# Transposing the gated convolution input, group A's output and the queries and keys on VectorE, quadrant by quadrant

## The chip, the cores and the metric

The kernel runs on one core of one Trainium2 chip. The metric is device time in microseconds (us) of one execution. TensorE (PE) multiplies matrices and writes to PSUM; VectorE (DVE) and ScalarE (ACT) work elementwise; GpSimd (POOL) does a few small powers; SyncE (SP) issues the DMAs. Each engine works through its own queue in order.

## The reference, cut to what matters

A trunk of two layers on a sequence of 256 tokens (two tiles of 128, here called token tiles) with 2048 channels in float32. Each layer:

```python
h = rmsnorm(x, norm_mix_pre[l])
proj = h @ w_in[l]                      # 2048 -> 5120 columns
a_q, a_k, a_v, b_glu, c_q, c_k, c_v, d_q, d_k, d_v = jnp.split(proj, split_at, axis=-1)
out_a = diff_attention(a_q, a_k, a_v, diff_lambda[l], diff_subln[l], l)   # 4 heads, rotary
out_b = conformer_conv(b_glu, conv_dw[l], ...)     # a*sigmoid(g), 31-tap depthwise conv, layernorm, silu, 512x512
out_c = gqa_axial_attention(c_q, c_k, c_v, ...)    # 4 query heads, 2 key heads
out_d = neighbourhood_attention(d_q, d_k, d_v, na_rpb[l])                 # 4 heads
mixed = jnp.concatenate([out_a, out_b, out_c, out_d], axis=-1) @ w_out[l]
x = x + rmsnorm(mixed, norm_mix_post[l])
h = rmsnorm(x, norm_ffn_pre[l])
f = (jax.nn.silu(h @ ffn_gate[l]) * (h @ ffn_up[l])) @ ffn_down[l]
x = x + rmsnorm(f, norm_ffn_post[l])
```

## The kernel before, in words

Every large product is made of three products of rounded float32 halves: high times high, high times low, low times high. A weight block of 128 rows by 1024 columns (a *unit*) is loaded, ACT writes its high half (`whi`), DVE the low half (`wlo`), and PE takes both. A *step* is one unit against one token tile: six matmuls of 128x512. Each layer goes through four phases in a fixed order of steps: the input projection (160 steps, in the column pairs B, C, A, D, V: `IN_ORDER`), the output projection (64 steps; its first half takes the groups' outputs in the order C, B, A, D: `OUT_ORDER`), gate and up, and down.

The order of all instructions is written by a planner while the kernel is built. `run` walks over the steps. Before each step it calls `fill` (convolution taps for DVE), `tick` (lets each running side job, a Python generator, go on to its next `yield`), `splits_to` (high and low halves, up to 7 units ahead) and `fill` again. `lhs` looks whether the left operand of the step has been made; as long as it hasn't, `wait` advances the planner's PE clock by 0.2 us and lets side jobs run, without a matmul of the step in between. So an output of group B that is late in the program stands ahead of all later steps on PE.

The planner keeps a clock for each engine in `spend` (lines 158 to 177). A DVE instruction is entered with 0.07 (or 0.13) us plus its elements per partition divided by 960, a PE transpose with 0.107 us. A side job may go on only when the planner's PE clock has passed the end of what it issued last plus 0.4 us (`LATENCY`, line 41). `fill` (line 339) issues taps only while DVE's clock is less than 1.5 us (`CONV_LEAD`, line 40) ahead of PE's.

The side jobs that the change touches:

- `glu` (line 644): after the column pair B, for each token tile, a times sigmoid(g); four PE transposes into a PSUM bank of the pool `tp`, an ACT copy into `uT`. When both token tiles are there, `conv` (line 671) issues the 31 taps for 4 channel blocks on DVE (`taps`), then for each token tile `conv_norm` (PE transposes, ACT, DVE, POOL, PE transposes, four ACT activations), then four products with `conv_pw`, which give `mixB`.
- `attn_a`, `attn_c`, `attn_d` (lines 808, 887, 958): after the column pairs A, C and D, `heads_transposed` turns queries and keys: per round one claim of a `tp` bank, four (or two) PE transposes, one ACT copy. There are 4 rounds in A, 4 in C (two of them of two blocks), 4 in D. Then the heads follow, at most two at a time.
- `out_a` (line 1013): when the four heads of A are done and the values V are there, for each token tile the products with the values, a norm, four PE transposes, and the split into `mixA`.

The pool `tp` has two PSUM banks; a job that finds both claimed yields until one is free.

`post` (line 541 and above) already turns the fourth quarter of x on DVE, as sixteen transposes of 32 partitions x 4 blocks x 32, four between two yields. The same form of instruction is what the change uses.

Of the kernel before, what the change touches and what calls it, by code (L numbers as in the profile page):

```python
# [13 lines left out]
AF = mybir.ActivationFunctionType  # L14
# [5 lines left out]
P = 128  # L20
L = 2
S = 256
T = S // P
# [7 lines left out]
PAD = TAPS // 2  # L31
# [71 lines left out]
class Trunk:  # L103
# [461 lines left out]
    def turned(self, l, j):  # L565
# [10 lines left out]
        for tok in range(T):  # L576
            self.mark("h", l, j, tok)


    def layer_consts(self, l):  # L580

        nc, a = self.nc, self.a
        lc = self.slot([2048], F32, "lc")
        v = self.v = {}
        self.l = l
        at = 0

        def part(n, shape):
            nonlocal at
            w = int(np.prod(shape))  # L590
            t = lc[:, at:at + w]
            at += w
            if len(shape) > 1:
                names = "abc"[:len(shape)]
                t = t.rearrange(f"p ({' '.join(names)}) -> p {' '.join(names)}", **dict(zip(names, shape)))
            v[n] = t
            return t

        for n in ("gqa_q_norm", "gqa_k_norm", "diff_subln"):
            part(n, (HD,))  # L600
        nc.sync.dma_start(lc[:, 0:at], a["heads"][l].partition_broadcast(P))
        first = at
        part("dw", (4, TAPS))
        for n in ("conv_dw_b", "conv_ln_g", "conv_ln_b", "conv_pw_b"):
            part(n, (4,))
        nc.sync.dma_start(lc[:, first:at], a["conv"][l])
        yield
        yield
        nc.vector.tensor_scalar(part("subln", (HD,)), v["diff_subln"], 1.0 - self.lam_init(l), None,
                                op0=ALU.mult)  # L610
        for n in ("q", "k"):
            g = v[f"gqa_{n}_norm"]
            cg, sg = part(f"cos_{n}", (T, HD)), part(f"sin_{n}", (T, HD))
            nc.vector.tensor_tensor(cg, self.rope["cos_c"], g.unsqueeze(1).to_broadcast([P, T, HD]),
                                    op=ALU.mult)
            gv = g.rearrange("p (b h w) -> p b h w", b=2, h=2)
            s4 = self.rope["sin_c"].rearrange("p t (b h w) -> p t b h w", b=2, h=2)
            o4 = sg.rearrange("p t (b h w) -> p t b h w", b=2, h=2)
            for h in range(2):
                for t in range(T):  # L620
                    nc.vector.tensor_tensor(o4[:, t, :, h], s4[:, t, :, h], gv[:, :, 1 - h], op=ALU.mult)
# [22 lines left out]
    def glu(self, phase, pair, tok):  # L644
        nc = self.nc
        if tok == 0:
            self.u = self.slot([T, 512], F32, "u")
            self.uT = self.slot([4, S + 2 * PAD], F32, "uT")
            nc.gpsimd.memset(self.uT[:, :, 0:PAD], 0.0)
            nc.gpsimd.memset(self.uT[:, :, PAD + S:], 0.0)  # L650
        av, gv = (self.acc[phase, pair, tok, b] for b in range(2))
        r = self.rstd[:, tok:tok + 1]
        u = self.u[:, tok]
        nc.scalar.activation(u, gv, AF.Sigmoid, scale=r)
        nc.vector.scalar_tensor_tensor(u, av, r, u, op0=ALU.mult, op1=ALU.mult)
        yield
        yield from self.claim("tp")
        b = self.bank("tp", (4, P))
        for c in range(4):
            nc.tensor.transpose(b[:, c], u[:, c * P:(c + 1) * P], self.ident)  # L660
        yield
        nc.scalar.activation(self.uT[:, :, PAD + tok * P:PAD + (tok + 1) * P], b, AF.Copy)
        yield
        self.free("tp")
        self.mark("u", phase)
        if tok == T - 1:
            yield from self.until(T, "u", phase)
            yield
            yield from self.conv()
# [103 lines left out]
            yield from self.until(T, "a", phase)  # L773
            yield from self.attn_a()

    def heads_transposed(self, dst, src, n):

        nc = self.nc
        for tok in range(T):
            yield from self.claim("tp")  # L780
            b = self.bank("tp", (4, P))
            for h in range(n):
                nc.tensor.transpose(b[:, h], src(tok)[:, h * P:(h + 1) * P], self.ident)
            yield
            nc.scalar.activation(dst[:, 0:n, tok * P:(tok + 1) * P], b[:, 0:n], AF.Copy)
            yield
            self.free("tp")

    def exps(self, p, src, nm, sm, scale):

        for t in range(T):
            self.nc.scalar.activation(p[:, t], src[:, t], AF.Exp, bias=nm[:, t:t + 1], scale=scale,
                                      accum_out=sm[:, t:t + 1])
# [14 lines left out]
    def attn_a(self):  # L808
        qk = self.slot([2, 4, S], F32, "qkA")
        for i in range(2):  # L810
            yield from self.heads_transposed(qk[:, i], lambda t: self.rotA[:, t, i], 4)
        self.ptA = self.slot([4, T, S], F32, "ptA")
        work = self.slot([2, 2, T, S], F32, "workA")
        for h in range(4):
            yield from self.until(h - 1, "done_a", self.l)
            self.spawn(self.head_a(h, qk, work[:, h % 2]))
            yield
# [68 lines left out]

    def attn_c(self):
        qk = self.slot([6, S], F32, "qkC")
        yield from self.heads_transposed(qk[:, 0:4], lambda t: self.rotC[:, t, 0:512], 4)
        yield from self.heads_transposed(qk[:, 4:6], lambda t: self.rotC[:, t, 512:768], 2)  # L890
        self.mixT[2] = self.slot([2, 4, S], F32R, "mixC")
        work = self.slot([2, 2, T, S], F32, "workC")
        for h in range(4):
            yield from self.until(h - 1, "mix_c", self.l)
            self.spawn(self.head_c(h, qk, work[:, h % 2]))
            yield
# [61 lines left out]
    def attn_d(self):  # L958
        qk = self.slot([2, 4, S], F32, "qkD")
        for i in range(2):  # L960
            yield from self.heads_transposed(qk[:, i], lambda t: self.rotD[:, t, i], 4)
        self.ptD = self.slot([4, T, S], F32, "ptD")
        work = self.slot([2, 2, T, S], F32, "workD")
        for h in range(4):
            yield from self.until(h - 1, "done_d", self.l)
            self.spawn(self.head_d(h, qk, work[:, h % 2]))
            yield
# [45 lines left out]
    def out_a(self):  # L1013
        nc, v = self.nc, self.v
        yield from self.until(4, "done_a", self.l)
        self.mixT[0] = self.slot([2, 4, S], F32R, "mixA")
        for t in range(T):
            yield from self.claim("sc")
            b = self.bank("sc", (4, HD))
            for h in range(4):  # L1020
                for c in range(T):
                    nc.tensor.matmul(b[:, h], self.ptA[:, h, c, t * P:(t + 1) * P],
                                     self.vAD[:, c, 0, h * HD:(h + 1) * HD], start=c == 0, stop=c == T - 1)
            yield
            ss, rs = self.small(4, "ss"), self.small(4, "rs")
            for h in range(4):
                self.square_sum(b[:, h], ss[:, h:h + 1], (HD,))
            self.rsqrt(rs, ss, 4, 1.0 / HD)
            o = self.tmp([4, HD], "oA")
            for h in range(4):  # L1030
                nc.vector.scalar_tensor_tensor(o[:, h], b[:, h], rs[:, h:h + 1], v["subln"],
                                               op0=ALU.mult, op1=ALU.mult)
            yield
            self.free("sc")
            yield
            yield from self.claim("tp")
            b = self.bank("tp", (4, P))
            for h in range(4):
                nc.tensor.transpose(b[:, h], o[:, h], self.ident)
            yield  # L1040
            self.split_hi_lo([self.mixT[0][:, i, :, t * P:(t + 1) * P] for i in range(2)], b)
            yield
            self.free("tp")
        self.mark("mix", self.l, 0)


# [134 lines left out]
```

## Time and profile before

| | us |
|---|---|
| median of 3 runs (2178.34 to 2178.55) | 2178.41 |
| the profiled execution | 2178.1 |
| its span from first to last instruction | 2175.9 |
| PE busy | 2154.6 (99%) |
| DVE busy | 1300.2 (60%) |
| ACT busy | 1092.4 (50%) |
| granted TensorE clock, mean | 0.999 |

PE is busy all the way; the other shares are means over phases that differ. In the slices of 100 us of the first layer's input projection DVE is busy for 94.3 of 100 us (100 to 200 us), in the feed-forward phases for 48 to 57. A line number says little here, since a helper records every compute instruction at line 89; so the rows are read by the names of the tiles.

### The profile page before, as it was taken

The page shows a single profiled execution, that of the slowest core. Times are in us where ns is not written, and L with a number is a line of the kernel's source. Part 1 is how long each engine was busy: PE and PEld are TensorE (multiplying, and loading weights), DVE is VectorE, ACT ScalarE, POOL GpSimd, SP SyncE. Part 2 cuts the span into 40 slices and gives each one's busy share as a digit, 9 for nine tenths or more (in the row PEclk, how much of TensorE's full clock was granted, in tenths as well). Part 3 has the DMA queues.
Part 4 walks back from the last instruction along what each step waited for, and adds up shares of the span by engine and source line. Part 5 has one row for each costly group of instructions (what it writes and reads, how often), then busy time and mean ns, then how long its engine had stood idle before and what let it go on. Part 6 is the DMA issues. An engine that isn't in the chain of part 4 may idle for free.

```text
span 2175.9 us, 25246 instructions
## 1 busy us (share of the span) xinstructions
PE 2154.6 (99%) x9696; PEld 1778.7 (82%) x9696; DVE 1300.2 (60%) x1616; ACT 1092.4 (50%) x1398; POOL 29.9 (1%) x38
## 2 busy tenths in 40 slices
PE   8999999999999999999999999999999999999998
PEld 7888888888888888888878888888888888888886
DVE  5898556755546554444488974566555555454444
ACT  6656755544445444343455577555444444443432
POOL 0000000000000000000000000000000000000000
PEclk9999999999999999999999999999999999999999
DMA  7556446776776666655565563557667666665553
GB/s 277 194 176 185 170 148 223 232 219 210 225 217 220 209 226 216 220 193 193 208 225 187 193 192 136 199 188 251 213 222 223 211 215 222 222 213 213 193 219 130
DMA packets 200281, 447.52 MB, mean 206 GB/s; under 512 B 20704, under 2 KB 43744, under 8 KB 197856
## 3 DMA queue, kind: packets, MB, share of 16 engines
q1 hardware_dynamic: 200016, 445.87, 60.9%
q8 instruction: 76, 1.25, 0.2%
q14 instruction: 45, 0.37, 0.1%
q10 hardware_dynamic: 144, 0.03, 0.0%
HBM read 425.93 MB, written 19.92 MB: 205 GB/s over the span
## 4 chain that ended last, share of the span: by engine, by line
PE 95%; ACT 2%; DVE 1%; issue 1%; DMA 1%; DVEq 0%; POOLq 0%; ACTq 0%; SPq 0%
PE acc L89 91%; PE tp L89 3%; PE sc L89 1%; ACT whi L89 1%; DVE wlo L89 1%; ACT workA L89 0%; DMA lc<-in_heads_dram 0%; ACT L89 0%; DVE mx L89 0%; ACT xT L89 0%; DVE xt L89 0%; DMA x<-in_x_dram 0%; ACT conv L89 0%; ACT junk L89 0%; DVE xT L89 0%
## 5 line engine op out<-in xcount | busy, mean ns | idle before, releaser
L89 PE MATMUL acc<-whi,xT 128*128 128x512 f32 x4096 | 1292.7, 393 | 5.4 <-ACT xT L89 2.4
L89 PEld LDWEIGHTS acc<-whi,xT 128*128 128x128 f32 x4096 | 770.0, 188 | 169.5 <-ACT xT L89 3.5
L89 PE MATMUL acc<-wlo,xT 128*128 128x512 f32 x2048 | 799.4, 390 | 2.6 <-DVE wlo L89 2.6
L89 ACT ACTIVATE whi<-raw,gains 128x1024 fp32r<-128x1024 f32 x512 | 580.5, 1150 | 365.3 <-PE acc L89 334.3
L89 DVE SCALAR_TENSOR_TENSOR wlo<-raw,gains,whi 128x1024 fp32r<-128x1024 f32 x512 | 641.7, 1278 | 188.9 <-ACT whi L89 180.9
L89 PEld LDWEIGHTS acc<-wlo,xT 128*128 128x128 f32 x2048 | 385.3, 188 | 81.9 <-DVE wlo L89 4.4
L89 DVE TENSOR_TENSOR wlo<-raw,whi 128x1024 fp32r<-128x1024 f32 x240 | 292.6, 1223 | 260.5 <-ACT whi L89 243.8
L89 PE MATMUL acc<-whi,hT 128*128 128x512 f32 x1408 | 434.1, 389 | 0.0
L89 ACT ACTIVATE whi<-raw 128x1024 fp32r<-128x1024 f32 x240 | 253.7, 1061 | 304.1 <-PE acc L89 304.0
L89 PEld LDWEIGHTS acc<-whi,hT 128*128 128x128 f32 x1408 | 264.3, 188 | 55.0
L89 PE MATMUL acc<-wlo,hT 128*128 128x512 f32 x704 | 273.9, 389 | 0.0
L89 PEld LDWEIGHTS acc<-wlo,hT 128*128 128x128 f32 x704 | 132.1, 188 | 27.3
L89 DVE TENSOR_TENSOR hT<-ht,hT 128x1024 fp32r<-128x1024 f32 x22 | 27.0, 1226 | 163.5 <-ACT hT L89 163.5
L89 DVE SCALAR_TENSOR_TENSOR h<-acc,rstd,h 128x512 f32<-128x512 f32 x44 | 33.1, 751 | 113.4 <-ACT h L89 113.4
L89 DVE SCALAR_TENSOR_TENSOR conv<-uT,lc,conv 128x256 f32<-128x256 f32 x240 | 99.4, 481 | 0.0
L89 ACT ACTIVATE hT<-ht 128x1024 fp32r<-128x1024 f32 x22 | 23.3, 1059 | 128.7 <-DMA ht<-h_blocks 128.7
L89 ACT ACTIVATE h<-acc,rstd 128x512 f32<-128x512 f32 x44 | 30.3, 689 | 80.5 <-PE acc L89 80.3
L89 ACT ACTIVATE junk<-acc 128x512 bf16<-128x512 f32 x32 | 19.0, 595 | 55.9 <-PE acc L89 53.0
L89 PE MATMUL acc<-whi,mixC 128*128 128x512 f32 x128 | 44.7, 402 | 0.0
L89 DVE TENSOR_TENSOR mg<-acc,gpost 128x512 f32<-128x512 f32 x32 | 21.3, 686 | 35.8 <-PE acc L89 19.5
L89 PE MATMUL acc<-whi,mixB 128*128 128x512 f32 x128 | 42.2, 397 | 0.0
L89 PE MATMUL acc<-whi,mixD 128*128 128x512 f32 x128 | 41.6, 391 | 0.0
(139 smaller groups left out, 987.4 us busy)
## 6 DMA issues: line engine op xcount, KB each, us to landing
raw<-in_ffn_gate_dram SPq DMA_DIRECT2D x176, 512.0 KB, 3.8
raw<-in_ffn_up_dram SPq DMA_DIRECT2D x176, 512.0 KB, 5.1
raw<-in_ffn_down_dram SPq DMA_DIRECT2D x88, 1024.0 KB, 5.0
raw<-in_w_in_dram SPq DMA_DIRECT2D x63, 1024.0 KB, 5.1
raw<-in_w_out_dram SPq DMA_DIRECT2D x32, 1024.0 KB, 5.0
raw<-in_w_in_dram SPq DMA_DIRECT2D x34, 512.0 KB, 4.7
h_blocks<-blocks SPq DMA_DIRECT2D x44, 256.0 KB, 5.5
ht<-h_blocks SPq DMA_DIRECT2D x88, 128.0 KB, 6.0
```

Source lines behind the costliest of these rows:

```text
L89: return f(*args, **kw)
```

## The change

The 32x32 transposes of DVE move a block from one quadrant of partitions to another; sixteen instructions turn four blocks of 128x128. A new helper does this, four instructions between two yields, and replaces the PE transposes and the ACT copies in `glu`, in `attn_a`, `attn_c` and `attn_d` (`heads_transposed` goes away) and, with a temporary `oT` in SBUF, the PE transposes in `out_a`.

```diff
+    def turn(self, dst, src):
+
+        src = src.rearrange("p (k n) -> p k n", n=P)
+        for q in range(4):
+            qs = slice(32 * q, 32 * q + 32)
+            for r in range(4):
+                rs = slice(32 * r, 32 * r + 32)
+                self.nc.vector.transpose(dst[qs, :, rs], src[rs, :, qs])
+            yield
...
-        yield from self.claim("tp")
-        b = self.bank("tp", (4, P))
-        for c in range(4):
-            nc.tensor.transpose(b[:, c], u[:, c * P:(c + 1) * P], self.ident)
-        yield
-        nc.scalar.activation(self.uT[:, :, PAD + tok * P:PAD + (tok + 1) * P], b, AF.Copy)
-        yield
-        self.free("tp")
+        yield from self.turn(self.uT[:, :, PAD + tok * P:PAD + (tok + 1) * P], u)
...
-            yield from self.heads_transposed(qk[:, i], lambda t: self.rotA[:, t, i], 4)
+            for t in range(T):
+                yield from self.turn(qk[:, i, :, t * P:(t + 1) * P], self.rotA[:, t, i])
...
-        yield from self.heads_transposed(qk[:, 0:4], lambda t: self.rotC[:, t, 0:512], 4)
-        yield from self.heads_transposed(qk[:, 4:6], lambda t: self.rotC[:, t, 512:768], 2)
+        for t in range(T):
+            yield from self.turn(qk[:, :, t * P:(t + 1) * P], self.rotC[:, t, 0:768])
...
-            yield from self.heads_transposed(qk[:, i], lambda t: self.rotD[:, t, i], 4)
+            for t in range(T):
+                yield from self.turn(qk[:, i, :, t * P:(t + 1) * P], self.rotD[:, t, i])
...
-            yield from self.claim("tp")
-            b = self.bank("tp", (4, P))
-            for h in range(4):
-                nc.tensor.transpose(b[:, h], o[:, h], self.ident)
-            yield
-            self.split_hi_lo([self.mixT[0][:, i, :, t * P:(t + 1) * P] for i in range(2)], b)
-            yield
-            self.free("tp")
+            ot = self.tmp([4, P], "oT")
+            yield from self.turn(ot, o.rearrange("p h w -> p (h w)"))
+            self.split_hi_lo([self.mixT[0][:, i, :, t * P:(t + 1) * P] for i in range(2)], ot)
+            yield
```

## Rows read from the trace of the kernel before

**Rows 1.** The page's chain that ended last, by line and tile.
```profile
PE acc L89 91%; PE tp L89 3%; PE sc L89 1%; ACT whi L89 1%; DVE wlo L89 1%; ACT workA L89 0%; DMA lc<-in_heads_dram 0%; ACT L89 0%; DVE mx L89 0%; ACT xT L89 0%; DVE xt L89 0%; DMA x<-in_x_dram 0%; ACT conv L89 0%; ACT junk L89 0%; DVE xT L89 0%
```
**Rows 2.** Busy time by stretch: length; PE, PEld, DVE, ACT, POOL (instructions); clock, DMA.
```profile
60.00:200.00 140.00, 140.00 (x645) 115.39 (x645) 129.59 (x234) 79.40 (x130) 3.80 (x2) 1.00 0.58 192
200.00:280.00 80.00, 79.82 (x399) 65.62 (x398) 43.68 (x74) 57.44 (x117) 2.13 (x3) 1.00 0.45 152
1141.00:1280.00 139.00, 139.00 (x641) 114.89 (x640) 129.49 (x228) 78.94 (x124) 3.79 (x2) 1.00 0.60 198
1280.00:1360.00 80.00, 79.95 (x400) 65.51 (x399) 43.04 (x77) 60.56 (x127) 3.10 (x3) 1.00 0.42 145
```
**Rows 3.** Timeline of PE about one round of transposes: start, us, instruction.
```profile
223.69 0.60 PE L89 MATMUL tp<-ident,rotD 128*128 128x128 f32 x4
224.04 0.48 PE L89 MATMUL acc<-whi,xT 128*128 128x512 f32 x1
224.36 0.40 PE L89 MATMUL acc<-wlo,xT 128*128 128x512 f32 x1
224.59 0.39 PE L89 MATMUL acc<-whi,xT 128*128 128x512 f32 x1
```
**Rows 4.** Groups of DVE instructions: busy us, mean ns of one.
```profile
L89 DVE STREAM_TRANSPOSE xt<-x 32x128 f32<-32x128 f32 x96 | 29.0, 303 | 1.5
```
**Rows 5.** Timeline of DVE while the fourth quarter of x is turned, layer 1.
```profile
1123.45 1.25 DVE L89 STREAM_TRANSPOSE xt<-x 32x128 f32<-32x128 f32 x4
1124.73 2.48 DVE L89 SCALAR_TENSOR_TENSOR wlo<-raw,gains,whi 128x1024 fp32r<-128x1024 f32 x2
1127.25 1.26 DVE L89 STREAM_TRANSPOSE xt<-x 32x128 f32<-32x128 f32 x4
...
1131.03 1.26 DVE L89 STREAM_TRANSPOSE xt<-x 32x128 f32<-32x128 f32 x4
```
**Rows 6.** Timeline of DVE: the last taps and the last part of mixB, both layers.
```profile
195.83 0.88 DVE L89 SCALAR_TENSOR_TENSOR conv<-uT,lc,conv 128x256 f32<-128x256 f32 x2
...
271.62 0.48 DVE L89 SCALAR_TENSOR_TENSOR mixB<-tp,lc,mixB 128x256 fp32r<-128x256 f32 x1
...
1273.40 2.06 DVE L89 SCALAR_TENSOR_TENSOR conv<-uT,lc,conv 128x256 f32<-128x256 f32 x5
...
1336.87 0.48 DVE L89 SCALAR_TENSOR_TENSOR mixB<-tp,lc,mixB 128x256 fp32r<-128x256 f32 x1 [2.92 <-ACT mixB L89]
```
**Rows 7.** Timeline of PE where the output projection takes up each group, both layers.
```profile
284.91 0.39 PE L89 MATMUL acc<-whi,mixB 128*128 128x512 f32 x1
...
298.10 0.39 PE L89 MATMUL acc<-whi,mixA 128*128 128x512 f32 x1
...
320.77 0.39 PE L89 MATMUL acc<-whi,mixA 128*128 128x512 f32 x1
...
1365.57 0.48 PE L89 MATMUL acc<-whi,mixB 128*128 128x512 f32 x1
...
1401.02 0.39 PE L89 MATMUL acc<-whi,mixA 128*128 128x512 f32 x1
```
**Rows 8.** Timelines of DVE and PE along group A, layer 0.
```profile
164.88 0.69 DVE L89 TENSOR_TENSOR rotA<-rotA,rope 128x512 f32<-128x512 f32 x1
...
191.71 1.14 PE L89 MATMUL sc<-qkA 64*128 64x256 f32 x8
...
292.87 0.69 DVE L89 TENSOR_TENSOR mixA<-tp,mixA 128x512 fp32r<-128x512 f32 x1 [2.12 <-ACT mixA L89]
```
**Rows 9.** Pieces of the way from taps to mixB: an ACT group, a PE round.
```profile
L89 ACT ACTIVATE conv<-tp,lc 128x128 f32<-128x128 f32 x16 | 6.0, 457 | 0.1
...
249.54 1.89 PE L89 MATMUL tp<-conv,pw 128*128 128x256 f32 x8
```
**Rows 10.** An early PE matmul; the stretch after the last matmul (columns of rows 2).
```profile
13.06 0.63 PE L89 MATMUL acc<-wlo,xT 128*128 128x512 f32 x1
...
2170.00:2176.00 6.00, 0.00 (x0) 0.00 (x0) 1.94 (x3) 0.00 (x0) 0.00 (x0) 0.63 0.48 176
```

More of the change, by code (lines that the diff above doesn't have):

```diff
@@ L774, in rope_a @@
             yield from self.attn_a()
-    def heads_transposed(self, dst, src, n):
-        nc = self.nc
-        for tok in range(T):
-            yield from self.claim("tp")
-            b = self.bank("tp", (4, P))
-            for h in range(n):
-                nc.tensor.transpose(b[:, h], src(tok)[:, h * P:(h + 1) * P], self.ident)
-            yield
-            nc.scalar.activation(dst[:, 0:n, tok * P:(tok + 1) * P], b[:, 0:n], AF.Copy)
-            yield
-            self.free("tp")
     def exps(self, p, src, nm, sm, scale):
@@ L1035, in out_a @@
             yield
-            yield from self.claim("tp")
-            b = self.bank("tp", (4, P))
-            for h in range(4):
-                nc.tensor.transpose(b[:, h], o[:, h], self.ident)
+            ot = self.tmp([4, P], "oT")
+            yield from self.turn(ot, o.rearrange("p h w -> p (h w)"))
+            self.split_hi_lo([self.mixT[0][:, i, :, t * P:(t + 1) * P] for i in range(2)], ot)
             yield
-            self.split_hi_lo([self.mixT[0][:, i, :, t * P:(t + 1) * P] for i in range(2)], b)
-            yield
-            self.free("tp")
         self.mark("mix", self.l, 0)
```

## The prediction

> **What bounds the kernel now.** I read the profile in this order: the chain that ended last, busy time by stretch, then timelines of PE and DVE about group B and group A. The chain is PE almost everywhere: the products into `acc` hold 91% of the span, all work in the `tp` banks 3% [rows 1]. So over the whole run a PE instruction taken away is time gained, as long as nothing else becomes late. The second view says where that may fail. From 60 to 200 us, the first layer's convolution taps, DVE is busy 129.6 of 140 us, in layer 1 129.5 of 139; right behind it, from 200 to 280 and from 1280 to 1360, only 43.7 and 43.0 of 80 [rows 2]. In the first stretch DVE has no room, because the planner pours taps into every gap; in the second it has some 36 us. The mean share of 60% hides both.
>
> Third, who must be in time. The last taps end at 196.7 and the last part of mixB at 272.1; PE takes up mixB at 284.9, a margin of 12.8 us. In layer 1 they are 1275.5, 1337.4 and 1365.6, a margin of 28.2 [rows 6, 7]. The second half of mixA is ready at 293.6 and is wanted at 298.1, a margin of 4.5 [rows 7, 8]. PE's program is in order: whichever group is late holds up all later steps.
>
> **What goes from PE.** Each layer has 2 rounds in glu, 4 in A, 4 in C (two of them short), 4 in D, 2 in out_a: 60 transposes, 15 full rounds of four, 30 in both layers. A round starts at 223.69 and the second matmul behind it at 224.36, 0.67 us, where one matmul takes 0.23 (224.36 to 224.59) [rows 3]; so a round costs 0.44 us of PE and 30 cost 13.2. Nothing covers that today, so it is the whole gain if nothing becomes late. The time from one transpose to the next is about 0.11 us. The Trainium skill (TensorE: Matmul & The Clock Gate, Part 4) gives some 275 ns for a transpose within a kernel; by that price 120 would be worth 33 us, but the trace's transposes overlap, and the row decides. ACT loses 28 copies of PSUM; it is on the chain with 1%, and I count nothing for that. The `tp` banks come free earlier for the convolution's rounds; worth between 0 and a few us on the way to mixB, which I use below.
>
> **What comes to DVE.** The same form of instruction is in the trace: 32x128, 303 ns [rows 4]; four of them and the start of the next instruction are 1.28 us apart (1123.45 to 1124.73), so 0.32 each [rows 5]. Per layer glu needs 2 turns of 16 (10.2 us), A 4 (20.5), D 4 (20.5), out_a 2 (10.2). C needs 2 turns with six blocks instead of four, 32 instructions; that size isn't in the trace. From below it costs 0.32 (10.2 us), from above 1.5 times as much (15.4); I take 0.39, half of the instruction as fixed (12.5). That is 73.9 us per layer, 148 in all, for 13 us of PE.
>
> **When the taps now end.** All but out_a's turns stand in the program before or among the taps: 10.2 + 20.5 + 20.5 + 12.5 = 63.7 us per layer. Taps come last in the planner's order of preference: they get what the turns and the low halves leave. DVE's free time from 60 to 280 is 10.4 + 36.3 = 46.7 us, from 1141 to 1360 it is 9.5 + 37.0 = 46.5 [rows 2]. So 17 us are lacking even if every gap is used. Some of the 43 us that are done there today (heads of A and D, what follows the taps) moves behind, since it depends on what is late: between 0 and the whole 17; I take 12, as heads of both groups are among it. Then the taps end at 280 + 5 = 285 and at 1365. (The planner enters a turn's instruction with 0.20 us, not 0.32, so it even issues more taps than fit, and low halves may come late; that I leave to the range.)
>
> **From the taps to mixB.** Before, it took 75.4 us in layer 0 and 61.9 in layer 1, with PE's steps between all rounds [rows 6]; that is the upper end. The lower end is the bare work: 8 ACT activations of 0.457, four PE rounds of 1.89, ACT and DVE behind each, 0.48 a piece: 15 us [rows 9]. Now PE will stand at the first mixB matmul, and the planner goes on in steps of 0.2 us, so it is nearer to the lower end. There are some twenty places where the jobs yield, with 0.4 us of the planner's latency each, 8 us, and some 5 for the statistics and norms: I take 28. mixB is ready at 313 and 1393, where PE took it up at 284.9 and 1365.6: 28.1 and 27.4 late.
>
> **The sum.** From the first mixB matmul to the second half took 35.9 and 35.4 us [rows 7]; about 3 of that are rounds of D and A, which now fall into the standing time. So +25.1 and +24.4, together +49.5 us. Of the 13.2 us saved nothing is left: PE reaches the wait earlier and stands longer. Against the profiled execution's 2178.1 (its span of 2175.9 and 2.2 around it; the median is 2178.4, the same within 0.02%) that is 2227.6, called 2228. What is queued behind the waiting matmul is the rest of the output projection, the norm and the feed-forward; nothing in them gives time back, as PE bounds them too.
>
> A stall has a price of its own: after the last matmul the granted clock of the stretch falls to 0.63, between the two levels of 2.4 and 1.2 GHz, and an early matmul lasts 0.63 us against 0.40 later [rows 3, 10]. About ten matmuls at the lower level after a stall would add 2.3 us in each layer. The Trainium skill (TensorE: Matmul & The Clock Gate, Part 1) says that an engine left idle falls to the lower level and has to work before it rises; by that rule the sum would be 2232. I leave it to the range, since the rounds for mixB keep PE partly at work.
>
> **The rivals.**
>
> *Only A is late.* In layer 1 groups of four turns stand 3.8 us apart (1123.45, 1127.25, 1131.03), because the planner lets a job go on only after its last work's end [rows 5]. A's 16 groups then take 61 us: its queries and keys are there at 165.6 + 61 = 226 instead of for scores at 191.7, 35 later [rows 8]. About 16 of that may go, as out_a waited for V anyway (estimate, bounds 0 and 20); out_a's own 8 groups bring about 6, the margin takes 4.5, and with PE standing jobs run faster (6): +14 per layer, 2206. For it: it needs no shortage of DVE. Against: B, by the sum above, is later still and covers it.
>
> *It all fits, and PE's gain stays.* 2178.1 - 13.2 = 2165. For it: margin 28 us for mixB in layer 1, ACT relieved, two `tp` banks for the convolution alone, so that 75 us from taps to mixB could become 45; it decides if then the taps end before 240 in layer 0. Against: A's margin of 4.5 us, and 43 of the 63.7 us come before or while the taps run in a stretch with 10 free.
>
> *Worse.* Low halves come late in C, A and D as well, since DVE is loaded beyond its time there, and the clock falls in both stalls: 15 to 30 more, about 2250.
>
> *About even.* Small stalls of 6 to 7 us in each layer that eat the gain: 2178.
>
> **How the numbers follow.** Forecast 0.52, only A late 0.20, worse 0.10, fits 0.13, about even 0.05. A measurement of this kernel tells 0.2%, 4.4 us, from no change. Faster 0.14 (fits, and a little of the even case), same 0.04, slower 0.82. The range runs from 2188 (A late by half of what I took, beside a B just in time) to 2252 (worse case's middle); it leaves out the two cases below, 0.18, and little above. The likeliest case's own range is 2210 to 2245: taps ending from 280 to 292 and 22 to 34 us behind them.
>
> **What the changed profile would show.** Right: 448 more DVE transposes with 0.30 to 0.40 us each; DVE about full from 60 to 280 and from 1141 to 1360; last taps after 260 in layer 0; gaps of PE of tens of us before the first mixB matmul in both layers, which name mixB's ACT or DVE as the one they wait for; feed-forward stretches of the same length as before. Wrong at the first step, if a round less shortens a stretch by other than 0.44 us; at the second, if taps end before 240; at the third, if PE waits for mixA or mixD and not for mixB. The forecast falls as a whole if PE stays busy through the output projection.

## The result, and the profile after

The changed kernel takes 2295.8 us (median of four runs, 2293.7 to 2296.7) against 2178.4: a ratio of 1.054, with an interval of 1.052 to 1.056. It is slower, as forecast, but by 117 us and not by 50; 2295.8 lies above the range, and above the case called "worse".

The page of the changed kernel: span, PE's busy time, and PE, DVE and PE's clock in 40 slices of 57 us.

```profile
span 2294.1 us, 25439 instructions
PE 2184.8 (95%) x9576; PEld 1789.1 (78%) x9576; DVE 1443.5 (63%) x2064; ACT 1077.8 (47%) x1368; POOL 28.9 (1%) x38
PE   8998859999999999999999987699999999999998
DVE  5997966765555555444489989557555555545544
PEclk9999969999999999999999998799999999999999
```

PE has 120 instructions less and yet is busy for 2184.8 us, where it was 2154.6; its idle time went from 21 to 109 us. The slices that fell are 4 to 6 and 24 to 26, the attention groups of each layer; the rest kept its length (from the second half of layer 1's output projection to the end, 774.9 us before and 774.5 after). The chain of the changed kernel shows who sets the pace there:

```profile
PE 76%; DVE 16%; ACT 3%; issue 2%; DMA 2%; SPq 0%; POOL 0%; DVEq 0%; POOLq 0%; ACTq 0%
PE acc L89 74%; DVE wlo L89 6%; DVE conv L89 3%; PE tp L89 2%; DVE qkD L89 2%; DMA raw<-in_w_in_dram 1%; DVE qkA L89 1%; DVE qkC L89 1%; ACT whi L89 1%; DVE mx L89 1%; PE sc L89 1%; ACT workD L89 1%; ACT L89 0%; DVE rope L89 0%; DVE rotC L89 0%
```

PE's `acc` products, 91% of the chain before [rows 1], are 74% now; DVE has 16%. The turns themselves, all 448 of them, in the groups of DVE instructions (busy us, mean ns of one):

```profile
L89 DVE STREAM_TRANSPOSE qkD<-rotD 32x128 f32<-32x128 f32 x128 | 38.7, 302 | 9.6 <-PE acc L89 7.7
L89 DVE STREAM_TRANSPOSE qkA<-rotA 32x128 f32<-32x128 f32 x128 | 38.7, 302 | 2.0
...
L89 DVE STREAM_TRANSPOSE qkC<-rotC 32x192 f32<-32x192 f32 x64 | 23.6, 369 | 0.9
L89 DVE STREAM_TRANSPOSE uT<-u 32x128 f32<-32x128 f32 x64 | 19.5, 304 | 1.0
L89 DVE STREAM_TRANSPOSE oT<-oA 32x128 f32<-32x128 f32 x64 | 19.3, 302 | 1.0
```

They last what [rows 4] said, and what the changed kernel's two loaded stretches look like is this (columns of rows 2: up to the last tap, then up to the last part of mixB; layer 0 in four rows, layer 1 in two):

```profile
60.00:200.00 140.00, 132.95 (x582) 109.19 (x581) 130.02 (x243) 65.23 (x90) 3.80 (x2) 0.99 0.58 190
200.00:280.00 80.00, 68.38 (x280) 52.90 (x279) 68.12 (x155) 32.50 (x50) 0.00 (x0) 0.91 0.39 133
280.00:307.90 27.90, 12.86 (x37) 8.00 (x38) 27.33 (x70) 12.66 (x35) 0.00 (x0) 0.60 0.43 149
307.90:351.30 43.40, 30.57 (x133) 23.63 (x132) 21.35 (x61) 28.28 (x78) 2.13 (x3) 0.78 0.00 0
1197.00:1444.70 247.70, 218.80 (x928) 175.94 (x929) 230.86 (x467) 117.53 (x180) 3.80 (x2) 0.93 0.51 172
1444.70:1484.60 39.90, 27.92 (x122) 21.35 (x121) 20.52 (x59) 29.05 (x78) 2.13 (x3) 0.77 0.00 0
```

From 60 to 307.9 DVE is busy 130.02 + 68.12 + 27.33 = 225.5 us of 247.9. PE, full in the same place before [rows 2], runs 85% from 200 to 280 and 46% from 280 to 307.9, at a granted clock of 0.60, between its two levels. The ends, in the timelines of DVE and PE, to be held against [rows 6, 7]:

```profile
307.41 0.48 DVE L89 SCALAR_TENSOR_TENSOR conv<-uT,lc,conv 128x256 f32<-128x256 f32 x1
350.80 0.48 DVE L89 SCALAR_TENSOR_TENSOR mixB<-tp,lc,mixB 128x256 fp32r<-128x256 f32 x1 [1.55 <-ACT mixB L89]
351.80 0.48 PE L89 MATMUL acc<-whi,mixB 128*128 128x512 f32 x1
384.54 0.39 PE L89 MATMUL acc<-whi,mixA 128*128 128x512 f32 x1
1444.17 0.48 DVE L89 SCALAR_TENSOR_TENSOR conv<-uT,lc,conv 128x256 f32<-128x256 f32 x1
1484.09 0.48 DVE L89 SCALAR_TENSOR_TENSOR mixB<-tp,lc,mixB 128x256 fp32r<-128x256 f32 x1
1486.71 0.58 PE L89 MATMUL acc<-whi,mixB 128*128 128x512 f32 x1
1519.55 0.39 PE L89 MATMUL acc<-whi,mixA 128*128 128x512 f32 x1
```

PE takes up mixB 0.5 us behind its last part in layer 0 (351.28 to 351.80) and 2.1 us behind it in layer 1, and from there on it runs without a gap (32.0 of 32 us from 352 to 384): group B decides, as forecast. The second half stands at 384.5 where it was 320.8 (+63.7), and at 1519.6 where it was 1401.0 (+118.5, so +54.8 in layer 1). That is all of the 118.2 us between the spans.

### The profile page after: what moved, and what is told of

Same layout as the page of the kernel before. It is cut to its first block, busy times and chain, and to the rows that moved or that the text cites. A ratio compares the mean times of both kernels' runs of the same rounds, so it can differ in the third digit from the quotient of the medians.

```text
span 2294.1 us, 25439 instructions
## 1 busy us (share of the span) xinstructions
PE 2184.8 (95%) x9576; PEld 1789.1 (78%) x9576; DVE 1443.5 (63%) x2064; ACT 1077.8 (47%) x1368; POOL 28.9 (1%) x38
## 4 chain that ended last, share of the span: by engine, by line
PE 76%; DVE 16%; ACT 3%; issue 2%; DMA 2%; SPq 0%; POOL 0%; DVEq 0%; POOLq 0%; ACTq 0%
PE acc L89 74%; DVE wlo L89 6%; DVE conv L89 3%; PE tp L89 2%; DVE qkD L89 2%; DMA raw<-in_w_in_dram 1%; DVE qkA L89 1%; DVE qkC L89 1%; ACT whi L89 1%; DVE mx L89 1%; PE sc L89 1%; ACT workD L89 1%; ACT L89 0%; DVE rope L89 0%; DVE rotC L89 0%
## 5 line engine op out<-in xcount | busy, mean ns | idle before, releaser
L89 PE MATMUL acc<-whi,xT 128*128 128x512 f32 x4096 | 1284.3, 393 | 17.3 <-ACT rotD L89 10.9
L89 PE MATMUL acc<-wlo,xT 128*128 128x512 f32 x2048 | 802.8, 392 | 20.4 <-DVE wlo L89 20.4
L89 DVE STREAM_TRANSPOSE qkD<-rotD 32x128 f32<-32x128 f32 x128 | 38.7, 302 | 9.6 <-PE acc L89 7.7
L89 PE MATMUL acc<-whi,mixD 128*128 128x512 f32 x128 | 41.6, 391 | 0.0
```

Source lines behind the costliest of these rows:

```text
L89: return f(*args, **kw)
```

## The experiments

Two questions. Why 117 and not 50: is it the *amount* of DVE work, or the *chain* (scores and taps now wait for something that stands in DVE's queue)? And what does each part cost alone? The dummy loads below put DVE work at the same places, but nobody waits for its results and TensorE keeps its transposes. (At A's output the load is issued within the job that makes it, which goes on only when the load has been issued; elsewhere it is a job of its own.) Before on the same chip took 2177.9 to 2178.2 each time.

| run | what | us | ratio (95%) | last tap, mixB, layer 0 |
|---|---|---|---|---|
| (after) | all five parts | 2295.8 | 1.052 to 1.056 | 307.9, 351.3 |
| r1_price | planner enters a turn with its real length | 2297.3 | 1.052 to 1.058 | 313.1, 346.6 |
| r2_load | light dummy load, 96 us of DVE | 2234.5 | 1.023 to 1.029 | 292.1, 315.1 |
| r3_burst | sixteen instructions in one go | 2286.3 | 1.047 to 1.053 | 320.7, 343.5 |
| r4_warm | PE kept busy in the wait | 2307.5 | 1.056 to 1.063 | 306.2, 350.9 |
| r5_load | dummy load of equal size, 144 us | 2270.7 | 1.041 to 1.045 | 313.2, 341.4 |
| r6_only_a | A alone on DVE | 2210.2 | 1.013 to 1.017 | 221.2, 276.8 |
| r8_only_d | D alone | 2191.7 | 1.004 to 1.008 | 196.3, 261.7 |
| r9_only_out | A's output alone | 2185.7 | 1.002 to 1.005 | 196.5, 271.9 |
| r10_only_glu | gated input alone | 2184.2 | 1.002 to 1.004 | 225.5, 293.9 |
| r11_half | half the dummy load, 72 us | 2207.6 | 1.012 to 1.016 | 238.3, 298.0 |
| r13_no_c | all but C | 2248.7 | 1.031 to 1.035 | 267.6, 310.5 |
| r14_ad_turn | A, D real; the rest as dummy load | 2283.2 | 1.046 to 1.051 | 293.6, 332.6 |

The us of DVE are the rise of its busy time over before (1300.2 to 1443.5 with the change).

**r1_price.** On the changed kernel:

```diff
+            if op == "transpose":
+                cost = 0.185 + n / 960
```

> The changed kernel, but the planner enters a DVE transpose with what it lasts: 0.185 us plus the elements of a partition over 960 (0.32 for 128 of them) instead of 0.07 plus the same (0.20). DVE's work is the same. If the amount of DVE work is the cause, the time stays within 12 us of the changed kernel's 2296 (2284 to 2308). If the wrong price is the cause (PE is given matmuls of side jobs too early and stands before them), a large part comes back: 2260 or less. If the spacing of a turn's four groups is the cause, it becomes worse, since the planner spaces them further: above 2305.

2297.3, where the amount as the cause had it: the planner's short price is not the cause.

**r2_load.** On the kernel before, spawned beside each part's own work:

```diff
+        n = 144 if src.shape[1] == 512 else 208
...
+                self.nc.vector.reduce_max(self.scratch[:, r:r + 1], self.all_tables[:, 0:n], axis=AX.X)
...
+        self.spawn(self.turns([self.rotA[:, t, i] for i in range(2) for t in range(T)]))
```

> The kernel before with all its PE transposes, and beside each turn that the change has, a side job that issues as many DVE instructions of the same length that nobody waits for (maxima over 144 or 208 elements of a constant table into one column, 0.30 and 0.37 us), four between two yields. No chain to queries, keys or the convolution's input is longer, PE loses nothing. Amount of DVE work as the cause: 2270 to 2310. Spacing (longer chains) as the cause: under 2210, since the chains are as before. Wrong price as the cause: as the amount, 2270 to 2310, since the price is as wrong here.

It cost 56 us, but the load was too light: these reductions start 0.21 us after one another, not 0.32. At 2234.5 it lies between the ranges of the theories and decides nothing; r5_load repeats it with a load of the right size.

**r3_burst.** On the changed kernel, one `yield` behind sixteen instructions and not behind each four:

```diff
                 self.nc.vector.transpose(dst[qs, :, rs], src[rs, :, qs])
-            yield
+        yield
```

> The changed kernel with one yield per turn instead of four: sixteen DVE transposes in a row. DVE's work is the same; queries and keys need a quarter of the planner's rounds. Amount as the cause: 2280 to 2310. Spacing as the cause: 2200 to 2245. Wrong price: about the same as the amount, and low halves later, 2290 to 2320.

2286.3, in the range of the amount and about 10 us back: the spacing of the turns is a small part. The taps end later (320.7) but mixB follows after 23 us and not 43; D's first scores start at 256.1, where they started at 304.8, so that less of A and D is left for that stretch.

**r4_warm.** On the changed kernel, products with a zero weight while the output projection waits:

```diff
+                if s.phase[0] == "out" and not s.first:
+                    bank = self.acc[s.phase, s.pair, s.tok, s.banks[0]]
+                    self.tc.nc.tensor.matmul(bank[0:64], self.zero, s.unit.hi[:, 0:512], start=False, stop=False)
```

> The changed kernel, but wherever the planner waits for a group's output in the output projection it also gives PE a matmul of 512 columns by a zero weight block of 64 columns into the accumulator (adds zero), so PE isn't idle and its granted clock should stay at the upper level. If the lower clock carries much of the loss, 2250 to 2275, and the granted clock in the waiting stretch rises from 0.75 to above 0.95. If the matmuls at the lower clock aren't on the chain (DVE is), 2285 to 2300 with the same clock.

Windows of this run (columns as above), from 268 to 308 and on to mixB:

```profile
268.00:308.00 40.00, 37.33 (x160) 24.74 (x157) 39.11 (x92) 13.29 (x36) 0.00 (x0) 0.91 0.45 158
308.00:353.00 45.00, 45.00 (x238) 33.01 (x237) 19.81 (x58) 28.81 (x83) 2.13 (x3) 1.00 0.00 1
```

The time, 2307.5, lies above both ranges. PE ran at the full clock behind the taps (1.00, where the changed kernel has 0.78), and mixB was there at 350.9, where it was 351.3. So in this stretch the lower clock is a consequence of the stall and not what makes mixB late. The run as a whole is 12 us longer, with 376 products more for PE.

**r5_load.** As r2_load, with more elements, and entered in the planner like a turn:

```diff
+        n, priced = (250, 128) if src.shape[1] == 512 else (313, 192)
...
+                self.spend("DVE", "transpose", priced, (), {})
```

> The kernel before, with TensorE's transposes kept, and beside them side jobs that give Vector as many instructions at the same places as the change does (reduce_max over 250 or 313 elements of the constant tables in place of a turn, nobody waits for the results), this time so long that one starts 0.32 or 0.39 us after the other, as the turns of the changed kernel do. The light version of this (r2_load, one every 0.21 us, about 96 us of Vector in all) cost 56 us. Theory 'volume': Vector has no such time, and the amount alone makes the convolution late; then nearly the whole loss is here, 2270 to 2300. Theory 'chain': the scores and the convolution now have to wait for Vector's full queue, and that makes up about half of the 117 us; then 2235 to 2255.

One group of four dummy reductions, and the windows of this run up to the last tap and up to mixB:

```profile
179.11 1.37 DVE L588 TENSOR_REDUCE scratch<-tables 128x1 f32<-128x250 f32 x4
180.39 0.87 DVE L89 SCALAR_TENSOR_TENSOR conv<-uT,lc,conv 128x256 f32<-128x256 f32 x2
```

```profile
60.00:313.20 253.20, 227.54 (x1015) 181.93 (x1014) 241.69 (x514) 132.06 (x239) 4.80 (x3) 0.95 0.48 163
...
313.20:341.40 28.20, 20.40 (x84) 16.99 (x83) 11.51 (x36) 12.08 (x33) 2.09 (x3) 0.73 0.00 0
```

Four take 1.28 us to the next start, as four turns do [rows 5]. The amount alone, with PE's 13.2 us of transposes still in, costs 92.5 us, where the change costs 117; 2270.7 is just inside the range of 'volume'. The taps end 5 us later than in the changed kernel (313.2), with more of the other groups' work done by then (241.7 us of DVE), and mixB follows after 28 us. The 25 us between the two runs are left for the chain, less than that theory wanted.

**r6_only_a, r8_only_d, r9_only_out, r10_only_glu.** The kernel before with `turn` and one hunk of the change each, as for A (for D with rotD, the two others as the change has them):

```diff
-            yield from self.heads_transposed(qk[:, i], lambda t: self.rotA[:, t, i], 4)
+            for t in range(T):
+                yield from self.turn(qk[:, i, :, t * P:(t + 1) * P], self.rotA[:, t, i])
```

> The kernel before with only group A's queries and keys turned by Vector (64 instructions per layer, 20.5 us). Theory 'threshold': the idle time of Vector between the convolution's start and the output projection (46.7 us per layer) takes in a part this small, and what is lost is what A's own heads are late: 2190 to 2225 (the prediction's rival of A alone gave 2206). Theory 'additive': each turn costs its share of the loss, 20.5 of 73.9 us, so 2178 + 0.28 x 117 = 2210, with taps ending about 25 us later in each layer.

> The kernel before with only group D's queries and keys turned by Vector (64 instructions per layer, 20.5 us), the last group to need them. Theory 'threshold': 2170 to 2190, since D's scores have the longest time and the taps behind still fit. Theory 'additive': 0.28 x 117 = 33 us, 2210, as for A.

> The kernel before with only group A's output turned by Vector (32 instructions per layer, 10.2 us), which all stand behind the taps. TensorE saves 2 rounds per layer, 1.8 us in all. Theory 'threshold': mixA's margin of 4.5 us in layer 0 decides; eight bursts of 1.28 us in place of eight copies and a PE round each: 2174 to 2186. Theory 'additive': 0.14 x 117 = 16 us, 2194.

> The kernel before with only the convolution's gated input turned by Vector (32 instructions per layer, 10.2 us), ahead of all taps. TensorE saves 2 rounds per layer, 1.8 us in all. Theory 'threshold' (Vector's idle time takes it in): taps start up to 10 us later in each layer but still end before 220 us, and mixB's margins of 12.8 and 28.2 us hold: 2174 to 2184. Theory 'linear' (every us of Vector here costs about 0.65 us, from the two dummy loads: 94 us cost 56, 150 us cost 92): 20.5 x 0.65 = 13 us, 2191.

Each of these four parts loses alone: 32.0, 13.5, 7.5 and 6.2 us. C alone was not run. In A's run mixB is on time (PE takes it up at 285.2) and PE waits for A: its second half starts 16.2 and 17.3 us later in the two layers. D (2.2 and 11.5 us later) and the output (4.0 and 2.3) are late in a like way, by less: D's scores stand at 270.5 and not at 247.3. With the gated input alone 10.2 us of turns end the taps 28.8 us later (225.5), 15 of them because the first tap starts at 83.6 and not at 68.5, and mixB is there 9 us behind the 284.9 at which PE took it before. A's 2210 is where both theories had it. The three small ones lie at the upper end of the threshold's range or just above, below what proportion wanted; but none keeps TensorE's gain, so a version with one part that beats the kernel before isn't among these four.

**r11_half.** r5_load with two reductions in place of four:

```diff
-            for r in range(4):
+            for r in range(2):
                 self.spend("DVE", "transpose", priced, (), {})
```

> The kernel before beside half of the matched dummy load (two reductions in place of four in each step, about 75 us of Vector in all, 37 per layer, which by the idle time of 46.7 us per layer should fit). Theory 'threshold': what fits in the gaps costs nothing, 2178 to 2190. Theory 'linear': the gaps of Vector cannot be used freely, and the loss goes on in proportion down to small loads: 75 x 0.65 less about 5 = 44 us, 2222.

29.6 us, between the two. Rise of DVE's busy time and cost of the three dummy loads are 72 and 29.6, 96 and 56, 144 and 92.5: a load that would fit in the idle time (36 us per layer, 46.7 idle) already costs 15 per layer, and from there each us costs 0.75 to 1.1. At this size, then, the room isn't free. Where the time goes can be read for layer 0: the taps end 41.6 us later (238.3), mixB is there 25.9 us later (298.0), 12.8 of these are its margin, and the 13 left are near the 14.1 us by which the second half starts later (334.87). And 36.3 of the 46.7 us idle lie behind 200 us [rows 2], after the last tap (196.7): a load ahead of the last tap can use them only by moving the taps, and with them all that waits for the taps.

**r13_no_c.** The changed kernel with C's hunk taken back:

```diff
-        for t in range(T):
-            yield from self.turn(qk[:, :, t * P:(t + 1) * P], self.rotC[:, t, 0:768])
+        yield from self.heads_transposed(qk[:, 0:4], lambda t: self.rotC[:, t, 0:512], 4)
+        yield from self.heads_transposed(qk[:, 4:6], lambda t: self.rotC[:, t, 512:768], 2)
```

> The changed kernel with only group C's queries and keys transposed by TensorE as before (12.5 us of Vector per layer less). Theory 'linear': 25 us x 0.65 = 16 us less, 2279. Theory 'threshold': beyond the point where the gaps are full each us counts once per layer, 25 us less or more, 2270 or below; taps end some 12 us earlier than 307.9.

2248.7: C is worth 47 us with 25 us of DVE. That is three times what 'linear' said, and 'threshold' holds it only because its range was open below; the taps end 40 us earlier (267.6), not 12. The other four together cost 70.8, the sum of what they cost alone being 59.2: nearly additive, until C comes on top.

**r14_ad_turn.** A's and D's hunks of the change, the dummy load at the places of the three others, as for C:

```diff
+        self.spawn(self.loads(T, 313, 192))
+        yield from self.heads_transposed(qk[:, 0:4], lambda t: self.rotC[:, t, 0:512], 4)
+        yield from self.heads_transposed(qk[:, 4:6], lambda t: self.rotC[:, t, 512:768], 2)
```

> Groups A and D turned by Vector as in the change; the gated input, group C and A's output transposed by TensorE as before, with the matched dummy load at their places. Vector has the same amount of work as in the changed kernel and in the run with the dummy load alone (2271). Theory 'late heads of A and D' (the 25 us beyond the amount come from scores that wait for Vector's full queue, so that A's and D's heads run at the same time as what follows the taps): 2285 to 2300, with 38 to 45 us from the last tap to the last part of mixB. Rival 'late start' (they come from the gated input's turns, which put the first tap 9 to 15 us later, and from group C): 2262 to 2278, with 24 to 30 us from the last tap to mixB.

Windows up to the last tap and up to mixB:

```profile
60.00:293.60 233.60, 208.06 (x910) 166.60 (x909) 225.15 (x463) 111.65 (x177) 3.79 (x2) 0.95 0.52 177
293.60:332.60 39.00, 26.84 (x118) 21.36 (x117) 20.44 (x61) 27.22 (x78) 2.13 (x3) 0.76 0.00 0
```

2283.2 lies between the two expectations, just under the first: of the 25 us of chain 12.5 come with A and D, by the difference to r5_load, and 12.6 with the three others. What A's and D's late scores do shows in the second row: 39 us from the last tap to mixB, 43 in layer 1, against 28 and 24 in r5_load, with 20.4 us of DVE and 27.2 of ACT in it, where r5_load has 11.5 and 12.1. And DVE did the same 225 us up to the last tap as in the changed kernel, but with 8.5 us idle and not 22.4. So most of that idle time hangs on C and the gated input (the output's turns stand behind the taps); without C alone, in r13_no_c, it is 12.7 us (194.9 us of DVE from 60 to 267.6).

## Why the prediction was right in its direction and wrong in its size

**Right.** What binds (PE everywhere, DVE without room in these two stretches), the price of the turns (302 ns, 0.32 from start to start), that B is the group that is late, that all of PE's gain is lost, that nothing behind the output projection gives time back. "Only A late" was the rival at 2206; A alone measured 2210, with 16.2 and 17.3 us per layer where the rival had 14. Its sum was right, though not each term (A's first scores came 45 us later, at 236.4, and not 35), and in the whole change it is covered by B, as the prediction said.

**Wrong, the first step: "When the taps now end".** The prediction had 225 us of DVE work from 60 us on, without a gap: 285. DVE did 225.5 us of work, but needed 247.9: the taps ended at 307.9. The failing assumption is "even if every gap is used". In the first stretch, 60 to 200, the gaps stayed: DVE is idle for 10.0 us, where it was idle for 10.4 [rows 2]. DVE's queue is in order; an instruction that has to wait holds all behind it. The waits of the changed kernel's DVE between 60 and 308 (us in total, times, longest):

```profile
DVE qkD L89 <- PE acc L89: 5.6, 1, 5.6
DVE wlo L89 <- ACT whi L89: 5.3, 2, 4.9
DVE mixC L89 <- ACT mixC L89: 3.9, 1, 3.9
DVE lambda L89 <- DMA lambda<-in_diff_lambda_dram: 3.0, 1, 3.0
```

These four are 17.8 of the 22.4 us; of the rest 3.5 is the time between turns (192 times 0.018, which the forecast had in its price). The first is a turn that stands at the head of DVE's queue until PE has made certain products:

```profile
215.01 1.24 DVE L89 STREAM_TRANSPOSE qkD<-rotD 32x128 f32<-32x128 f32 x4 [5.56 <-PE acc L89]
```

Its input isn't what is late, since the last of `rotD` was written at 205.7, and PE works all through this wait. By the order of the program these products are the last that read the first quarter of the projection's input, and `qkD` probably takes its place in the shared pool; no run tests that. PE's waits from 160 to 352 in the same run:

```profile
PE acc L89 <- DVE wlo L89: 9.8, 4, 6.4
PE tp L89 <- DVE workA L89: 8.6, 2, 5.4
PE acc L89 <- ACT rotD L89: 5.7, 1, 5.7
PE sc L89 <- DVE conv L89: 4.9, 1, 4.9
PE tp L89 <- ACT conv L89: 3.9, 2, 2.4
```

So the shortage bites from 193 us on, in weights' low halves and in softmax, long before mixB is due, and each engine's wait makes the next one of the other. One such wait starts at the weights. In the timelines, first the changed kernel, then the last two lines the kernel before:

```profile
167.21 11.78 SPq L646 DMA_DIRECT2D bias<-in_na_rpb_rev_dram  x16
179.09 6.20 SPq L214 DMA_DIRECT2D raw<-in_w_in_dram  x6
188.04 2.19 ACT L89 ACTIVATE whi<-raw,gains 128x1024 fp32r<-128x1024 f32 x2 [11.63 <-DMA raw<-in_w_in_dram]
189.22 1.28 DVE L89 SCALAR_TENSOR_TENSOR wlo<-raw,gains,whi 128x1024 fp32r<-128x1024 f32 x1 [4.86 <-ACT whi L89]
198.78 0.79 PE L89 MATMUL acc<-whi,xT 128*128 128x512 f32 x1 [5.73 <-ACT rotD L89]
...
164.69 11.83 SPq L636 DMA_DIRECT2D bias<-in_na_rpb_rev_dram  x16
185.22 1.15 ACT L89 ACTIVATE whi<-raw,gains 128x1024 fp32r<-128x1024 f32 x1 [0.34 <-DMA raw<-in_w_in_dram]
```

SyncE (SPq) issues sixteen loads of group D's bias before the next weight loads, in both kernels. Before, these weights came just in time; now ACT stands 11.6 us for them and DVE 4.9 us for ACT, with taps and C's softmax behind it in its queue. In layer 1 ACT's wait of this kind is 8.9 us. In r5_load the longest is 1.1 in layer 0 and 6.5 in layer 1, and without C (r13_no_c) none in either layer is longer than 2.3, with the bias loads at the same place. The prediction has no term for this. It put all of PE's loss into one gap before mixB and left the low halves to the case "worse". That one gap isn't there either: no single wait of PE in the list is longer than 6.4 us, and PE is busy for 30.6 of the 43.4 us between the last tap and mixB. That these particular waits are the cause of the late taps is read from the trace; taking them away one by one was not tried. The dummy loads show by size that idle time is no free room: 36 us per layer ought to fit and cost 15.

**Wrong, the second step: "From the taps to mixB".** Forecast 28, measured 43.4 and 39.9 (351.3 less 307.9, 1484.6 less 1444.7). The 12 us of DVE work that the forecast pushed behind the taps was pushed there, but taken as free: in layer 0 this stretch holds 9.8 us more of DVE and 16.2 more of ACT than in r5_load. Those heads of A and D run in the same queues as the convolution's norms and rounds. Where they come earlier (r3_burst, r5_load) the same way takes 23 and 28 us, so 28 was about right for a tail without them.

**The sum by these two terms,** layer 0: 22.9 and 15.4 us too little, 38.3 together; the forecast had +25.1, the measurement is +63.7, a difference of 38.6. In layer 1: the stretch before the last tap is 16 us too short (1141 moved by the 63.7 is 1204.7, and 1444.7 less that is 240 and not 224), the tail 12: 28 of 30.4 us.

**The clock** was estimated at 2.3 us per layer. PE's busy time rose by 30.2 us with 13.2 us of transposes gone, and matmuls in the stalls start 0.43 us apart (199.37 to 199.80) and not 0.23 [rows 3]. The granted clock there is 0.50, the lower of the two levels (columns of rows 2):

```profile
198.70:201.50 2.80, 2.72 (x6) 1.96 (x7) 2.79 (x6) 2.35 (x5) 0.00 (x0) 0.50 0.00 0
```

r4_warm removes that behind the taps, and mixB comes no earlier. That supports leaving the clock out of the sum for this stretch; what it costs in the stalls before the last tap was not tested.

**The amount** by itself makes 79% of the loss (92.5 of 117); the rest is put down to the chain. What stays open is why C's share is that large: r14_ad_turn has C's amount without its chain and lies 34.5 us above the run without C, so most of it is the amount that comes on top of a full queue, but the other two parts were changed there as well. The late weight loads are a candidate: ACT's longest waits for one in the two layers are 11.6 and 8.9 us with the whole change, 3.9 and 6.8 in r14_ad_turn, and at most 2.3 without C. No run takes them away alone.

The Trainium skill (VectorE: DVE Perf Modes, The three transpose paths) gives 311 ns for Vector and 390 ns for TensorE on a 128x128 tile of bf16 and adds that Vector only turns blocks of 32x32. Its rules for kernel authors, on the same page, send a 128x128 transpose to TensorE. The runs agree with that rule, and show the size in float32: sixteen quadrant turns, which do make full transposes, are 5.1 us of DVE for four 128x128 blocks, where PE's round is 0.44 us [rows 3].

## What to carry to other kernels

Idle time of an engine with an in-order queue is not a store that a new load can draw on: here 36 us of load per layer into 46.7 us of gaps cost 15 us per layer. Ask where the gaps lie, and what a late instruction holds back. Work that is pushed behind the critical step is not free either, since it then runs beside the step that everything waits for. And when a share of busy time is read, ask for it stretch by stretch: DVE's mean of 60% held two stretches of 93%, and these set the price.

## What the runs showed of the hardware

- The turns' stream transposes do not overlap with their successor: 302 ns long and 0.32 us from start to start, 369 ns and 0.385 us for 32x192. Other instructions of DVE do overlap: reductions of 405 ns start 0.32 us apart (r5_load), taps of 480 ns 0.40 apart. It isn't the operation as such: a stream transpose over all 128 partitions, in the feed-forward, is 0.70 us long and the next instruction starts after 0.63 (r13_no_c). Of a turn's four instructions in a row each reads another quadrant than the one before it, and these others don't; which difference decides was not tested.

```profile
446.77 0.70 DVE L89 STREAM_TRANSPOSE blocks<-h 128x512 f32<-128x512 f32 x1
447.40 2.44 DVE L89 SCALAR_TENSOR_TENSOR wlo<-raw,gains,whi 128x1024 fp32r<-128x1024 f32 x2
```

- So two groups with equal busy time can take unequal time, and a dummy load has to be matched by its starts. The Trainium skill (VectorE: DVE Perf Modes, The DRAIN you can't avoid) says that the next operation does not start until the pipe is empty, and that one which is not held starts earlier. The trace has both: the turns' transposes by the first, the others by the second.
- Keeping PE busy through a stall restores its clock (1.00 against 0.78, r4_warm) and brought mixB no earlier here (350.9 against 351.3).
